# A decoder trunk's gate projections by seven products: first product seeded into the accumulating banks, Silu in one activation, two quarters by products in the last z pair

## Chip, cores and metric

The kernel runs on one core of a Trainium2 chip. The metric is the device time of one execution in microseconds (us), the median over several runs. The engines in the texts are TensorE (PE in the profile; its weight loads are PEld), VectorE (DVE), ScalarE (ACT), GpSimd (POOL, here above all the issuer of one DMA queue) and SyncE (SP, which issues the weight loads).

## What is computed

Two layers over 256 tokens of width 2048. The first mixes by a gated linear recurrence (HGRN2) and an RG-LRU, the second by an mLSTM. The change lies in the second layer: `og` and `z` are two 2048 x 2048 projections of the normalised input, which gate the mLSTM's output before its output projection.

```python
hn = rmsnorm(h, o_norm[j])
u = hn @ o_w_in[j]                     # q,k | v | og | z | ig | fg
...
yc = mlstm(q, k, v.reshape(bsz, s, C_HEADS, C_DV), li, lf)
yc = (head_rmsnorm(yc, c_norm[j]) * jax.nn.sigmoid(og.astype(jnp.float32))
      * jax.nn.silu(z.astype(jnp.float32)))
mix = yc.astype(h.dtype) @ o_w_out[j]
h = h + mix
pl = rmsnorm(p[i].astype(h.dtype) @ ple_w[i], ple_norm[i])
h = h + jax.nn.sigmoid(h @ ple_gate_w[i]) * pl
```

All of it is float32. A product of two float32 matrices is made of three passes: each operand is split into a high part and the rest (`hi`, `lo`), and hi x hi, hi x lo and lo x hi are added up in one PSUM bank.

## The kernel before

**Products.** A projection takes its output in blocks: 512 output columns (index `j`) by 128 tokens (index `hf`, two halves) fill one PSUM bank. The contraction over 2048 inputs is cut into four quarters (`kq`), each with a 128 x 2048 weight block that comes as two 512 KB pieces. A piece is loaded by an SP transfer into a `raw` buffer (five of them), cast to its high part `whi` on ScalarE (line 135, or 206 for pieces loaded elsewhere) and subtracted to its low part `wlo` on VectorE (line 136 or 207); there are four `whi` and four `wlo` buffers. A quarter for both token halves is 24 matmuls of 128 x 128 by 512 columns (`plain`, line 223).

**Seven products.** `seven` (line 262) makes two output blocks `j`, `j + 1` at once. For the quarters in `kqs` it treats the two token halves, the two input halves (`side`) and the two output blocks as a 2 x 2 by 2 x 2 matrix product and forms it with seven products in place of eight (Strassen's scheme in Winograd's form). The combinations of activations (`qs`, by `combos`) are made once beforehand; the combinations of weights are made in the call, in the buffers X, Y, Z (and W). With two quarters, X and Y are pairs of tiles from `chain2` (tag `qk`, four buffers), and the sums with a block still in DRAM are made by transfers on the POOL queue that add to the tile (`add_loaded`, line 288). With one quarter they are single tiles from `chain` (tag `ch`, two buffers) and the sums are VectorE additions (`add`). The quarters in `rest` go by `plain`. A product on one quarter has 6 matmuls, on two 12.

**Banks.** A call uses four PSUM banks: A, E and B from the pool `pm` (tag `mm`, three banks) and F from `px` (tag `mx`, three banks). The first product, A11 times B11, is part of all four outputs: A goes on accumulating into output (0, 0), and a copy of the product, `p1`, is kept in SBUF and added to or subtracted from what B, F and E hold later on, by `soon` on VectorE (line 292). `p15` and `g` are the other two SBUF halves that collect partial sums. The four results leave the generator one after another: (0, 0) from A, (0, 1) from `p15`, (1, 0) from `g`, (1, 1) from `p1`.

**Callers.** `pair` (line 1338) starts a call; its last argument says whether two quarters go by products. There are four calls in a row: og for blocks 0 and 1 (one quarter), og for blocks 2 and 3 (two), z for 0 and 1 (two), z for 2 and 3 (one). Each og result passes a Tanh on ScalarE (line 1349), which later multiplies the mLSTM's numerator (`mixed_gates`). Each z result passes a Tanh (line 1363) and a VectorE product (line 1364): (tanh(z/2) + 1) z is twice silu(z), and the factor 1/4 in `fac` (line 1298), with the norm's scale, makes up for both gates. Line 1368 multiplies with the mLSTM's result. When both halves of a block are there, `feature_major` (started as lane `fm0` to `fm3`) turns it: VectorE transposes (line 648), a transfer to DRAM and four back on the POOL queue (lines 635 and 638), then scaling and splitting. After the fourth call come the per-layer embedding (`embed`, matmuls of line 472) and the output projection, which reads what the lanes made.

**Order.** The program is written in one order and a planner orders each engine's instructions by priority and by when it expects their inputs. `high_priority(offset=n)` puts instructions as if written n places earlier: 400 for the weight splits and `add`, 450 for `soon` and the copy of A, 100 for the z gates. `pump` advances each lane by one step; it stands within `plain`, between the token halves, and at some places in `seven`. An instruction that waits holds up those behind it on its engine or queue.

Of the kernel before, what the change touches and what calls it, by code (L numbers as in the profile page):

```python
# [11 lines left out]
F32 = mybir.dt.float32  # L12
# [3 lines left out]
AF = mybir.ActivationFunctionType  # L16
ALU = mybir.AluOpType
PSUM = bass.MemoryType.PSUM

P = 128  # L20
# [23 lines left out]
def trunk(ctx: ExitStack, tc: tile.TileContext, a, out):  # L44
    nc = tc.nc
    v, s, gp, te, sy = nc.vector, nc.scalar, nc.gpsimd, nc.tensor, nc.sync
# [176 lines left out]
    def plain(w, j, kq, act, ps, first=(False, False), end=False):  # L223

        parts = load_weights(w[4 * j + kq])
        for hf in range(2):
            product(ps[hf], stationary(act, (2 * kq, 2 * kq + 1), hf), parts, first[hf], end)
            if hf == 0:
                pump()
# [32 lines left out]
    def seven(w, j, act, qs, kqs, room, part):  # L262

        def src(b, side, kq):
            return block(w[4 * (j + b) + kq], side * 1024, 1024)

        def load(tile_of, b, side):
            tiles = []
            for kq in kqs:
                t = tile_of()  # L270
                sy.dma_start(out=t, in_=src(b, side, kq))
                tiles.append(t)
            return tiles

        def ring():
            return wp.tile([P, 1024], F32, name="raw", tag="raw", bufs=5)

        def split(tiles):
            return [split_weights(t) for t in tiles]

        def add(x, y):
            with tc.high_priority(offset=400):
                for xi, yi in zip(x, y):
                    v.tensor_tensor(out=xi, in0=xi, in1=yi, op=ALU.add)

        def add_loaded(x):
            for xi, kq in zip(x, kqs):
                gp.dma_start(out=xi, in_=src(1, 0, kq), accum_op=ALU.add)

        def soon(out, in0, in1, op):  # L290
            with tc.high_priority(offset=450):
                v.tensor_tensor(out=out, in0=in0, in1=in1, op=op)

        def quadrant(side, hf):
            return stationary(act, [2 * kq + side for kq in kqs], hf)

        def combo(n):
            return [[t for kq in kqs for t in qs[n, kq][x]] for x in range(2)]

        two = len(kqs) == 2  # L300
        rest = [kq for kq in range(4) if kq not in kqs]
        A, E, B = (pm.tile([P, 512], F32, name="mm", tag="mm") for _ in range(3))
        F = px.tile([P, 512], F32, name="mx", tag="mx")
        p1, p15, g = part(), part(), part()
        X = load(room, 0, 0)
        product(A, quadrant(0, 0), split(X), True)
        if two:
            add_loaded(X)
        with tc.high_priority(offset=450):
            s.copy(p1, A)  # L310
        Y = load(room, 1, 1)
        product(E, combo(4), split(Y), True)
        if not two:
            W = load(ring, 1, 0)
            add(Y, W)
            add(W, X)
        plain(w, j, rest[0], act, (A, F), first=(False, True))
        product(B, combo(1), split(X if two else W), True)
        add(X, Y)
        if two:  # L320
            add_loaded(Y)
        soon(p15, B, p1, ALU.add)
        if not two:
            plain(w, j, rest[1], act, (A, F))
            product(B, combo(2), split(X))
            soon(g, B, p1, ALU.subtract)
        pump()
        Z = load(ring, 0, 1)
        product(A, quadrant(1, 0), split(Z))
        if not two:  # L330
            add(X, Z)
        plain(w, j, rest[-1], act, (A, F))
        yield 0, 0, A
        if two:
            product(B, combo(2), split(X))
            add(X, Z)
            soon(g, B, p1, ALU.subtract)
            product(F, quadrant(1, 1), split(X), end=True)
            pump()
        product(B, combo(3), split(Y))  # L340
        soon(p15, B, p15, ALU.subtract)
        if not two:
            product(F, quadrant(1, 1), split(X), end=True)
        soon(p15, F, p15, ALU.subtract)
        pump()
        yield 0, 1, p15
        for kq in rest:
            plain(w, j + 1, kq, act, (E, B), end=(kq == 3))
        soon(g, E, g, ALU.add)
        yield 1, 0, g  # L350
        soon(p1, B, p1, ALU.subtract)
        yield 1, 1, p1

    def newton(y, t, r, yh):
        v.tensor_scalar(t.bitcast(I32), y.bitcast(I32), 1, None, op0=ALU.logical_shift_right)
# [265 lines left out]
    norm = {}  # L621
# [506 lines left out]
    with tc.tile_pool(name="m1", bufs=2) as m1:  # L1128
# [156 lines left out]
        def mix_norm():  # L1285


            t, r, yh = (m1.tile([P, 16], F32, name=n, bufs=1) for n in ("nwt", "nwr", "nwy"))
            s.activation(den, den, AF.Abs)
            v.tensor_tensor(out=den.rearrange("p (h n) -> p h n", h=2), in0=den.rearrange("p (h n) -> p h n", h=2),  # L1290
                            in1=aT[:, 1, :, 0:8], op=ALU.max)
            v.tensor_scalar(den, den, 1e21, EPS ** 0.5, op0=ALU.min, op1=ALU.mult)
            v.tensor_tensor(out=den, in0=den, in1=den, op=ALU.mult)
            v.scalar_tensor_tensor(den, ss, 1.0 / 256, den, op0=ALU.mult, op1=ALU.add)
            newton(den, t, r, yh)
            for hf in range(2):
                c = slice(hf * 8, hf * 8 + 8)
                v.tensor_scalar(fac[:, c], r[:, c], norm["rt"][:, hf:hf + 1], 0.25, op0=ALU.mult, op1=ALU.mult)
            yield

        qs = {}
# [25 lines left out]
        def part():  # L1327
            n = len(turn) % 4
            turn.append(n)
            return store_of[n // 2][:, n % 2 * 512:(n % 2 + 1) * 512]  # L1330
# [7 lines left out]
        def pair(w, jj, two):  # L1338
            return seven(w, jj, acth, qs, (0, 1) if two else (0,), chain2 if two else chain, part)
# [17 lines left out]
        pact = load_p()  # L1357
        for jj in (0, 2):
            us = [m1.tile([P, 2, 512], F32, name="u", tag="vt", bufs=6) for _ in range(2)]
            for b, hf, src in pair(a["oz"], jj, not jj):  # L1360
                j, u = jj + b, us[b]
                with tc.high_priority(offset=100):
                    s.activation(u[:, hf], src, AF.Tanh, scale=norm["rth"][:, hf:hf + 1])
                    v.scalar_tensor_tensor(u[:, hf], u[:, hf], 1.0, src, op0=ALU.add, op1=ALU.mult)
                for i in range(2):
                    c = hf * 8 + 2 * j + i
                    e = slice(i * 256, (i + 1) * 256)
                    v.scalar_tensor_tensor(u[:, hf, e], u[:, hf, e], fac[:, c:c + 1], nums[j][:, hf, e],
                                           op0=ALU.mult, op1=ALU.mult)
                if hf:  # L1370
                    start(f"fm{j}", feature_major(u, "cn", 4 * j, y, 5))
# [114 lines left out]
        rest = last_chunk()  # L1486
# [153 lines left out]
```

## Time and profile before

| | us |
|---|---|
| median of 3 runs (1028.17 to 1028.58) | 1028.18 |
| profiled execution, whole time | 1028.08 |
| its span, first to last instruction | 1026.3 |
| TensorE busy | 1016.2 (99%) |
| VectorE busy | 794.4 (77%) |
| ScalarE busy | 623.1 (61%) |
| mean DMA rate over the span | 235 GB/s |
| mean granted TensorE clock | 0.997 |

The page's chain of work that ended last is 97% TensorE. Matmuls overlap: a row's duration (0.39 us) is longer than the distance between two starts, and a busy TensorE means that matmuls followed one another without a gap, not how fast they ran. Times in rows of a timeline are counted from the span's start. In brackets at a row's end stands how long the engine had been idle before it and which instruction ended that.

### The profile page before, as it was taken

Reading aid. Unit: us, or ns where it says so; the run is one execution under the profiler, and the core shown is the slowest. Engines: PE = TensorE matmul, PEld = TensorE weight load, DVE = VectorE, ACT = ScalarE, POOL = GpSimd, SP = SyncE. Lnnn points to the kernel's source line nnn. Section 1 sums busy time; section 2 is a strip of 40 time slices with the busy share of each in tenths; the row PEclk is TensorE's granted clock in tenths of the full one; section 3 lists DMA queues with packets and bytes.
Section 4 is the critical chain, followed back from the end, with each engine's and each line's share of the span. In section 5 each row is a group of like instructions: output and inputs, shape, how many; then the busy total and the mean of one; then the engine's idle time right before and its main releaser. Section 6 shows DMA issues by size and latency. Waiting matters only on the chain.

```text
span 1026.3 us, 14463 instructions
## 1 busy us (share of the span) xinstructions
PE 1016.2 (99%) x5194; PEld 843.8 (82%) x5194; DVE 794.4 (77%) x1180; ACT 623.1 (61%) x893; POOL 101.7 (10%) x186
## 2 busy tenths in 40 slices
PE   9999999999999999999999999999999999999996
PEld 7888888888888888888888888888888888888886
DVE  7858968969685775767559997888999986766684
ACT  7675554686974344565457876665666667344562
POOL 0111101011112121021021100000011112111000
PEclk9999999999999999999999999999999999999998
DMA  9887757567688897697798755376875789887652
GB/s 361 331 240 237 221 175 203 169 200 231 228 264 276 290 292 234 225 308 259 221 288 255 228 184 189 124 245 194 278 173 170 234 275 329 250 275 258 219 185 82
DMA packets 69384, 241.09 MB, mean 235 GB/s; under 512 B 8992, under 2 KB 10400, under 8 KB 69312
## 3 DMA queue, kind: packets, MB, share of 16 engines
q1 hardware_dynamic: 55008, 194.41, 58.0%
q0 software_dynamic: 13872, 45.23, 15.7%
q8 instruction: 40, 0.66, 0.3%
q10 hardware_dynamic: 432, 0.52, 0.1%
q14 instruction: 32, 0.26, 0.1%
HBM read 220.21 MB, written 19.92 MB: 234 GB/s over the span
## 4 chain that ended last, share of the span: by engine, by line
PE 97%; ACT 1%; DMA 1%; DVE 1%; issue 0%; ACTq 0%; DVEq 0%
PE mm L196 21%; PE mm L197 21%; PE mm L198 21%; PE mm L217 12%; PE mx L198 4%; PE mx L196 4%; PE mx L197 4%; PE mx L217 3%; PE nu L1276 1%; PE mm L472 1%; DMA raw<-in_pw_dram 1%; PE mm L1466 1%; PE mm L1464 1%; PE mm L1465 1%; PE mx L785 0%; DVE wlo L136 0%
## 5 line engine op out<-in xcount | busy, mean ns | idle before, releaser
L136 DVE TENSOR_TENSOR wlo<-raw,whi 128x1024 fp32r<-128x1024 f32 (+1 forms) x333 | 401.6, 1214 | 156.6 <-ACT whi L135 147.7
L135 ACT CAST whi<-raw 128x1024 fp32r<-128x1024 f32 (+1 forms) x333 | 348.1, 1048 | 268.0 <-PE mm L198 183.5
L196 PE MATMUL mm<-whi,ahl 128*128 128x512 f32 x960 | 375.1, 391 | 0.0
L197 PE MATMUL mm<-wlo,ahl 128*128 128x512 f32 x960 | 374.0, 390 | 0.2 <-DVE wlo L136 0.2
L198 PE MATMUL mm<-whi,ahl 128*128 128x512 f32 x960 | 373.6, 389 | 0.0
L196 PEld LDWEIGHTS mm<-whi,ahl 128*128 128x128 f32 x960 | 180.2, 188 | 38.1 <-issue 0.8
L197 PEld LDWEIGHTS mm<-wlo,ahl 128*128 128x128 f32 x960 | 180.2, 188 | 37.6 <-DVE wlo L136 0.9
L198 PEld LDWEIGHTS mm<-whi,ahl 128*128 128x128 f32 x960 | 180.3, 188 | 37.6
L217 PE MATMUL mm<-whi,ahl 128*128 128x512 f32 x288 | 91.1, 389 | 0.0
L217 PEld LDWEIGHTS mm<-whi,ahl 128*128 128x128 f32 x288 | 54.1, 188 | 11.2
L196 PE MATMUL mx<-whi,ahl 128*128 128x512 f32 x160 | 62.2, 389 | 0.0
L197 PE MATMUL mx<-wlo,ahl 128*128 128x512 f32 x160 | 62.2, 389 | 0.0
L198 PE MATMUL mx<-whi,ahl 128*128 128x512 f32 x160 | 62.2, 389 | 0.0
L217 PE MATMUL mm<-wlo,ahl 128*128 128x512 f32 x144 | 56.3, 391 | 0.3 <-DVE wlo L136 0.3
L207 DVE TENSOR_TENSOR wlo<-ch,whi 128x1024 fp32r<-128x1024 f32 x34 | 41.0, 1220 | 6.0 <-ACT whi L206 5.4
L206 ACT CAST whi<-ch 128x1024 fp32r<-128x1024 f32 x34 | 35.6, 1052 | 6.4 <-PE mm L217 3.4
L197 PEld LDWEIGHTS mx<-wlo,ahl 128*128 128x128 f32 x160 | 30.1, 188 | 6.3
L196 PEld LDWEIGHTS mx<-whi,ahl 128*128 128x128 f32 x160 | 30.1, 188 | 6.2
L198 PEld LDWEIGHTS mx<-whi,ahl 128*128 128x128 f32 x160 | 30.0, 188 | 6.2
L217 PE MATMUL mx<-whi,ahl 128*128 128x512 f32 x104 | 34.4, 390 | 0.0
L217 PEld LDWEIGHTS mm<-wlo,ahl 128*128 128x128 f32 x144 | 27.0, 188 | 6.5 <-DVE wlo L136 1.0
L217 PE MATMUL mm<-whi,q 128*128 128x512 f32 x96 | 32.1, 389 | 0.0
(370 smaller groups left out, 1110.7 us busy)
## 6 DMA issues: line engine op xcount, KB each, us to landing
raw<-in_ew_dram SPq DMA_DIRECT2D x64, 512.0 KB, 5.1
raw<-in_g_dram SPq DMA_DIRECT2D x64, 512.0 KB, 4.9
raw<-in_eo_dram SPq DMA_DIRECT2D x32, 512.0 KB, 5.5
raw<-in_oqk_dram SPq DMA_DIRECT2D x32, 512.0 KB, 4.8
raw<-in_ov_dram SPq DMA_DIRECT2D x32, 512.0 KB, 4.4
raw<-in_oo_dram SPq DMA_DIRECT2D x32, 512.0 KB, 4.9
raw<-in_oog_dram SPq DMA_DIRECT2D x24, 512.0 KB, 4.5
raw<-in_oz_dram SPq DMA_DIRECT2D x24, 512.0 KB, 4.7
```

The source lines that it names most:

```text
L135: last["act"] = s.copy(h, r).ins
L136: last["dve"] = v.tensor_tensor(out=l, in0=r, in1=h.bitcast(F32), op=ALU.subtract).ins
L196: te.matmul(ps[hf], xh, wh, start=(k == 0), stop=False)
L197: te.matmul(ps[hf], xh, wl, start=False, stop=False)
L198: last["pe"] = te.matmul(ps[hf], xl, wh, start=False, stop=(k == KT - 1)).ins
L206: last["act"] = s.copy(hi, r).ins
L207: last["dve"] = v.tensor_tensor(out=lo, in0=r, in1=hi.bitcast(F32), op=ALU.subtract).ins
L217: last["pe"] = te.matmul(o, x, y, start=(first and k + i == 0), stop=(end and k == n - 1 and i == 2), skip_group_check=True).ins
L472: last["pe"] = te.matmul(ps[hf][:, o:o + w_], tokens(pact[x], k, hf), (hi, lo)[y][:, k * 512 + o:k * 512 + o + w_], start=(n == mine[0]), ...
L1276: te.matmul(ps[:, 0:n], x[:, i, o:o + P], y[:, b, i], start=(b == 0 and x is sh and y is vh), stop=(b == hf and y is vl))
L1464: te.matmul(o, xh, wh, start=(k == 0), stop=False)
L1465: te.matmul(o, xh, wl, start=False, stop=False)
```

## The change

It has three parts.

- In `seven`, A moves to the pool `px`, and F, E and B take the three banks of `pm`. After the first product ScalarE copies A into F and its negative into B, and no later product starts those banks anew, so both go on accumulating on top. With that, `p1` is gone; `b5` (for `p15`) and `g` take plain copies of B on ScalarE (`keep`), two VectorE steps stay for `b5` and one for `g`, and result (1, 1) is read from B itself. This holds for all four calls.
- The z gates pass one Silu on ScalarE with the norm's scale in place of Tanh and the VectorE product; `fac` is set to half of `r`.
- The last call, z for blocks 2 and 3, puts two quarters through products in place of one.

```diff
@@ -291,6 +291,10 @@
+        def keep(out, bank):
+            with tc.high_priority(offset=450):
+                s.copy(out, bank)
@@ -299,31 +303,32 @@
-        A, E, B = (pm.tile([P, 512], F32, name="mm", tag="mm") for _ in range(3))
-        F = px.tile([P, 512], F32, name="mx", tag="mx")
-        p1, p15, g = part(), part(), part()
+        A = px.tile([P, 512], F32, name="mx", tag="mx")
+        F, E, B = (pm.tile([P, 512], F32, name="mm", tag="mm") for _ in range(3))
+        b5, g = part(), part()
...
         with tc.high_priority(offset=450):
-            s.copy(p1, A)
+            s.copy(F, A)
+            s.activation(B, A, AF.Copy, scale=-1.0)
...
-        plain(w, j, rest[0], act, (A, F), first=(False, True))
-        product(B, combo(1), split(X if two else W), True)
+        plain(w, j, rest[0], act, (A, F))
+        product(B, combo(1), split(X if two else W))
...
-        soon(p15, B, p1, ALU.add)
+        keep(b5, B)
...
-            soon(g, B, p1, ALU.subtract)
+            keep(g, B)
...
-        soon(p15, B, p15, ALU.subtract)
+        soon(b5, B, b5, ALU.subtract)
...
-        soon(p15, F, p15, ALU.subtract)
+        soon(b5, F, b5, ALU.subtract)
         pump()
-        yield 0, 1, p15
+        yield 0, 1, b5
...
-        soon(p1, B, p1, ALU.subtract)
-        yield 1, 1, p1
+        yield 1, 1, B
@@ -1295,7 +1299,7 @@
-                v.tensor_scalar(fac[:, c], r[:, c], norm["rt"][:, hf:hf + 1], 0.25, op0=ALU.mult, op1=ALU.mult)
+                v.tensor_scalar(fac[:, c], r[:, c], 0.5, None, op0=ALU.mult)
@@ -1357,11 +1361,10 @@
-            for b, hf, src in pair(a["oz"], jj, not jj):
+            for b, hf, src in pair(a["oz"], jj, True):
                 j, u = jj + b, us[b]
                 with tc.high_priority(offset=100):
-                    s.activation(u[:, hf], src, AF.Tanh, scale=norm["rth"][:, hf:hf + 1])
-                    v.scalar_tensor_tensor(u[:, hf], u[:, hf], 1.0, src, op0=ALU.add, op1=ALU.mult)
+                    s.activation(u[:, hf], src, AF.Silu, scale=norm["rt"][:, hf:hf + 1])
```

More of the change, by code (lines that the diff above doesn't have):

```diff
@@ L336, in seven @@
             add(X, Z)
-            soon(g, B, p1, ALU.subtract)
+            keep(g, B)
             product(F, quadrant(1, 1), split(X), end=True)
```

## The prediction

> **What bounds the kernel now.** I read the page's busy shares first, then the table of engines by stretch over the four `seven` calls and the embedding that follows them, then TensorE's timeline at the joints.
>
> ```profile
> PE 1016.2 (99%) x5194; PEld 843.8 (82%) x5194; DVE 794.4 (77%) x1180; ACT 623.1 (61%) x893; POOL 101.7 (10%) x186
> ```
>
> ```profile
> core 0: us, PE busy (x) PEld busy (x) DVE busy (x) ACT busy (x) POOL busy (x), PEclk, DMA share, GB/s
> 661.96:707.47 45.51, 45.51 (x216) 38.22 (x214) 39.83 (x67) 27.53 (x43) 1.77 (x2) 1.00 0.69 221
> 707.47:748.85 41.38, 41.09 (x181) 33.72 (x180) 36.22 (x35) 27.00 (x29) 3.37 (x4) 1.00 0.79 230
> 748.85:789.65 40.80, 40.80 (x181) 33.80 (x180) 40.30 (x43) 25.85 (x27) 2.25 (x3) 1.00 0.63 177
> 789.65:832.00 42.35, 42.35 (x187) 34.84 (x186) 39.14 (x49) 27.31 (x37) 5.55 (x10) 1.00 0.75 244
> 832.00:842.88 10.88, 10.88 (x49) 9.01 (x48) 10.85 (x16) 7.71 (x10) 2.18 (x4) 1.00 0.85 251
> ```
>
> The columns are length, then busy time with instruction count for each engine. The first four stretches are the calls in order: oog pair 0 (one quarter by products), oog pair 2 (two quarters), oz pair 0 (two), oz pair 2 (one). TensorE is busy throughout at a granted clock of 1.00, so the kernel's time is its count of matmuls times their pitch, plus the few places where it waits. VectorE is nearly as full (40.30 of 40.80 us in call 3); ScalarE is two thirds full. I found the joints in the timeline:
>
> ```profile
> 663.32 0.39 PE L217 MATMUL mm<-whi,q 128*128 128x512 f32 x1
> ...
> 664.68 0.39 PE L217 MATMUL mm<-whi,ahl 128*128 128x512 f32 x1
> ...
> 710.19 0.39 PE L217 MATMUL mm<-whi,q 128*128 128x512 f32 x1
> ...
> 751.57 0.39 PE L217 MATMUL mm<-whi,q 128*128 128x512 f32 x1
> ...
> 759.73 0.39 PE L217 MATMUL mm<-whi,q 128*128 128x512 f32 x1
> ...
> 791.01 0.39 PE L217 MATMUL mm<-whi,q 128*128 128x512 f32 x1
> ...
> 832.00 0.39 PE L472 MATMUL mx<-whi,ahl 128*128 128x512 f32 x1
> ```
>
> Each call's first `whi,q` row is the start of product E; product A stands before it with 6 matmuls (one quarter) or 12 (two). Call 3 holds 180 matmuls from 748.85 to 789.65: 40.80 / 180 = 0.2267 us each. That is the pitch; the 0.39 of a row is the pipelined length.
>
> **What each call loses now.** Call 4 has 186 matmuls, 42.16 us at that pitch, and takes 42.35: 0.19 lost. Call 2 has 180 and takes 41.38: 0.58 lost. Call 1 has 186 and the last `mix` products besides, so its loss can't be read off. Call 3 loses nothing. Call 2's loss has a row:
>
> ```profile
> 714.94 0.50 PE L217 MATMUL mm<-wlo,ahl 128*128 128x512 f32 x1 [0.29 <-DVE wlo L136]
> ```
>
> The late `wlo` was VectorE's last in an unbroken row of work:
>
> ```profile
> 708.52 1.23 DVE L207 TENSOR_TENSOR wlo<-ch,whi 128x1024 fp32r<-128x1024 f32 x1 [1.79 <-ACT whi L206]
> 709.66 0.68 DVE L292 TENSOR_TENSOR pr<-mm,pr 128x512 f32<-128x512 f32 x1
> 710.27 1.22 DVE L207 TENSOR_TENSOR wlo<-ch,whi 128x1024 fp32r<-128x1024 f32 x1
> 711.40 1.22 DVE L136 TENSOR_TENSOR wlo<-raw,whi 128x1024 fp32r<-128x1024 f32 x1
> 712.53 1.22 DVE L1343 SCALAR_TENSOR_TENSOR num<-tho,num 128x1024 f32<-128x1024 f32 x1
> 713.67 1.22 DVE L136 TENSOR_TENSOR wlo<-raw,whi 128x1024 fp32r<-128x1024 f32 x1
> ```
>
> **The change part by part.** *Seven products on two quarters in call 4.* One quarter: 7 products of 6 and 6 `plain` quarters of 24, 186. Two: 7 of 12 and 4 of 24, 180. Six matmuls go: 6 x 0.2267 = **1.36 us**, on TensorE, so on the path. Call 4 then has the form of call 3, whose loss is nil, so I also count its 0.19 as gone (bounds 0 and 0.19). It adds three weight splits (22 for 19), each one cast on ScalarE and one subtraction on VectorE, the costliest rows of the page:
>
> ```profile
> L136 DVE TENSOR_TENSOR wlo<-raw,whi 128x1024 fp32r<-128x1024 f32 (+1 forms) x333 | 401.6, 1214 | 156.6 <-ACT whi L135 147.7
> L135 ACT CAST whi<-raw 128x1024 fp32r<-128x1024 f32 (+1 forms) x333 | 348.1, 1048 | 268.0 <-PE mm L198 183.5
> ```
>
> So 3 x 1.05 = 3.1 us on ScalarE and 3 x 1.21 = 3.6 us on VectorE; the VectorE additions of weight tiles stay at four. It also reads two more 512 KB blocks (18 for 16), 1 MB in 41 us on top of 244 GB/s, about 270: the DMA share goes from 0.75 to some 0.83, and the stretch after it runs at 0.85 with TensorE full. Four of its transfers become accumulating ones on the POOL queue (the second rival). Its X and Y tiles now come from the ring of four that call 3 uses, and must wait for call 3's last splits; calls 2 and 3 share that ring in the same way today and the start of call 3 loses nothing.
>
> *First product into the banks.* Per call one ScalarE copy of A (L310) becomes two, and two of the six VectorE evictions (L292, `b5` and `g` by `keep`) become ScalarE copies; the last one, `p1 = B - p1`, goes altogether. VectorE loses 3 x 0.68 = 2.1 us per call, ScalarE gains 3 x 0.57 = 1.7 us, by these rows:
>
> ```profile
> L310 ACT COPY pr<-mm x4: 559/568/587, 663.7 to 791.5; 128x512 f32<-128x512 f32 x4
> L292 DVE TENSOR_TENSOR pr<-mm,pr x20: 650/684/692, 673.9 to 834.2; 128x512 f32<-128x512 f32 x20
> L1364 DVE SCALAR_TENSOR_TENSOR u<-u,pr x6: 681/687/694, 783.1 to 836.5; 128x512 f32<-128x512 f32 x6
> L1363 ACT ACTIVATE u<-pr,rth x6: 718/724/725, 782.4 to 834.9; 128x512 f32<-128x512 f32 x6
> ```
>
> No row has a copy from bank to bank; I take 0.57 (from bank to SBUF), between 0.47 (the spacing of two ScalarE starts below) and 0.72 (L1363, which reads SBUF and a scale). The Trainium skill, "ScalarE: Activation LUTs", under "Step-by-step: what each stage is for", says that ScalarE reaches PSUM with less latency than SBUF; by it each copy costs at most 0.57, and no run here shows it yet.
>
> In call 2 the eviction at 709.66 is the one that goes. Every later VectorE start moves up by its 0.61 us (709.66 to 710.27). The late `wlo` was due at 714.50, seven matmuls after 710.19 + 12 x 0.2267 = 712.91, and came 0.44 later; it is then in time. The 0.29 goes; the rest of the 0.58 is a slow restart behind it, so the gain is 0.3 to 0.58 and I take 0.3, the recorded idle time.
>
> *The new wait.* Bank A can't be added to until both copies have read it; behind the waiting matmul stands all of TensorE. Call 1 is the tight one, because E there has only 6 matmuls:
>
> ```profile
> 663.69 0.59 ACT L310 COPY pr<-mm 128x512 f32<-128x512 f32 x1
> 664.16 1.07 ACT L206 CAST whi<-raw 128x1024 fp32r<-128x1024 f32 x1
> ...
> 711.01 0.57 ACT L310 COPY pr<-mm 128x512 f32<-128x512 f32 x1
> ...
> 752.04 0.56 ACT L310 COPY pr<-mm 128x512 f32<-128x512 f32 x1
> ```
>
> The copies follow at 0.47 us (663.69 to 664.16), so the second would end at 664.16 + 0.59 = 664.75, and A's next matmul is due at 664.68: with a semaphore about 0.2 us late. I take **+0.2**, between 0 (F's copy is the only one) and 1.0 (a cast comes between the two). In call 2 the second copy ends at 712.05 and A is due at 712.91; in call 3 at 753.1 against 754.29. These wait for nothing.
>
> *One Silu for Tanh and a VectorE product.* Eight L1364 go, 8 x 0.69 = 5.5 us of VectorE over calls 3 and 4; ScalarE's count stays. Call 3 then has 40.30 - 2.1 - 2.8 = 35.4 us on VectorE, call 4 39.14 + 3.6 - 2.1 - 2.8 = 37.8 of 40.8, and ScalarE 27.3 + 3.1 + 1.7 = 32.1 at most. No VectorE time is on the path but in call 2, so I count nothing. The function is new to the kernel, so a table load comes with it; the trace has this one:
>
> ```profile
> 1018.20 1.28 ACT L1434 ACT_TABLE_LOAD   x1
> 1019.50 0.20 ACT L1434 ACTIVATE warm<-th 128x1 f32<-128x1 f32 x1
> ...
> 768.09 0.69 ACT L1363 ACTIVATE u<-mm,rth 128x512 f32<-128x512 f32 x1 [1.67 <-PE mm L217]
> ```
>
> The first z activation at 768.09 stands behind 1.67 us of idle ScalarE, which holds 1.28 us; cost nothing, and at most 1.28 if the load is held with its activation. Whether a second load follows for the later Tanh no row tells; I count it as covered too. The Trainium skill, "ScalarE: Activation LUTs", under "What ACT_TABLE_LOAD costs", speaks against this part: 1283 ns for the load, which the row confirms, and about 1380 ns of drain, which no row here shows (the next activation starts 1.30 us after the load did). By it a switch is 2.66 us, 1.0 us more than the idle time, and the sum would be 1.0 us higher if nothing else hid it.
>
> **Sum.** The profiled execution took 1028.08 us, 1026.3 of it the span; the three runs' median is 1028.18, so the two agree within 0.1. 1028.08 - 1.36 - 0.19 - 0.3 + 0.2 = **1026.4 us**. Past the calls TensorE's order is the same and the tail after its last matmul is untouched, so all of it arrives at the end.
>
> **The rivals.** *ScalarE hands it back.* If the planner puts a weight cast between the two copies of A, call 1 waits 1.0 and call 2 about 0.2 (711.01 + 0.47 + 0.95 + 0.57 = 713.0 against 712.91, and the semaphore). Against the forecast's +0.2 that is 1.0 more: **1027.4**, and up to 1028.2 with an exposed table load. For it: ScalarE runs back to back at 711 (the Tanh before the copy). Against: the copies have the higher priority.
>
> *The accumulation stuck on POOL (slower).* Call 4's X tiles are now added to by POOL transfers, and POOL's queue at that time also carries the first z pair's way through DRAM:
>
> ```profile
> 744.91 0.85 POOL L288 DMA_DIRECT2D ch<-in_oz_dram  x1 [24.11 <-DVE wlo L207]
> 746.26 0.84 POOL L288 DMA_DIRECT2D ch<-in_oz_dram  x1 [0.50 <-DVE wlo L207]
> ...
> 787.95 0.56 POOL L635 DMA_DIRECT2D ducn<-w  x1 [26.84 <-DVE w L648]
> 791.14 2.24 POOL L638 DMA_DIRECT2D r<-ducn  x4 [2.64 <-DMA ducn<-w]
> ```
>
> ```profile
> ch<-in_oz_dram POOLq DMA_DIRECT2D x4, 512.0 KB, 6.1
> hq<-dh POOLq DMA_DIRECT2D x4, 512.0 KB, 13.8
> ```
>
> Moved on by call 3's 40.8, the two accumulations are due at 785.7 and 787.1, a hair before L635. If the planner puts L635 and the four L638 ahead of them, they leave at 793.4 and land 6.1 us later, 799.5; cast 1.05 and subtraction 1.21 make 801.8. TensorE wants that tile at 759.73 + 40.8 = 800.5, so it waits 1.3, and 2.4 with the second tile, which lands 1.1 later: **1028.8**, slower than before. It is slower by more than 0.2% from landings of about 7.5 us on; at 13.8, which the queue's other row shows, it would be 1036. Against it: due times that let both accumulations go first.
>
> *More relief.* If both losses go whole (0.58 + 0.19) and call 1 doesn't wait, 1028.08 - 1.36 - 0.77 = **1025.95**, less what call 1 loses now.
>
> **How the numbers follow.** A measurement of this kernel can tell about 0.2%, 2.06 us, from no change: faster is below 1026.1, slower above 1030.2. The forecast has 0.56 with its own range 1025.9 to 1026.9, of which 0.24 lie below 1026.1 and 0.32 within. ScalarE's return has 0.18 (within), POOL's queue 0.15 (0.10 slower, 0.05 within), more relief 0.11 (faster). That makes faster 0.35, within 0.55, slower 0.10. The range 1025.6 to 1029.0 takes in all of these and the POOL case at its usual landing, with 0.35 under the case of more relief for call 1; about 0.15 stays outside.
>
> **What would show it.** Right: 5188 matmuls for 5194, calls 2 to 4 of 40.8 us, no wait at call 2's first `plain`, one more table load, no L1364 group, at most 0.3 us of wait on the ScalarE copy of A in call 1. Wrong: TensorE idle behind a `wlo` or a POOL transfer at call 4's B product; a call longer than its count times 0.2267; L638 ahead of L288 on POOL; or a length change outside 662 to 832.

## The result and the profile after

The changed kernel takes **1026.91 us** (median of 22 runs, 1026.11 to 1027.66) and the kernel before, run beside it, 1028.57 us (22 runs). The ratio is 0.9982, with a 95% interval of 0.9976 to 0.9989: a gain of 0.18%, which is within the 0.2% that counts as no change here, at the side of faster. The forecast was 1026.4.

The profiled execution of the changed kernel took 1026.88 us with a span of 1025.1 and a mean granted clock of 0.998. Its page has the busy shares:

```profile
PE 1015.3 (99%) x5188; PEld 843.8 (82%) x5188; DVE 787.6 (77%) x1163; ACT 632.2 (62%) x909; POOL 105.2 (10%) x190
```

There are 5188 matmuls, six fewer than before, as foreseen. The table of engines by stretch, over the same four calls and the embedding behind them:

```profile
core 0: us, PE busy (x) PEld busy (x) DVE busy (x) ACT busy (x) POOL busy (x), PEclk, DMA share, GB/s
661.90:708.54 46.64, 45.80 (x215) 38.14 (x214) 38.86 (x65) 28.94 (x46) 1.79 (x2) 1.00 0.63 194
708.54:749.58 41.04, 41.04 (x182) 33.67 (x180) 34.62 (x32) 28.09 (x32) 3.37 (x4) 1.00 0.80 231
749.58:790.38 40.80, 40.80 (x182) 33.80 (x180) 37.38 (x39) 28.55 (x31) 4.81 (x7) 1.00 0.84 243
790.38:831.18 40.80, 40.80 (x182) 33.80 (x180) 39.49 (x45) 31.62 (x42) 5.99 (x11) 1.00 0.83 229
831.18:842.06 10.88, 10.88 (x50) 9.01 (x48) 10.11 (x14) 7.17 (x10) 3.24 (x6) 1.00 0.94 271
```

The first number after the colon is the length. Set it against before: call 1 went from 45.51 to 46.64 (**+1.13**), call 2 from 41.38 to 41.04 (−0.34), call 3 stays at 40.80, call 4 went from 42.35 to 40.80 (**−1.55**). So calls 2 and 4 gained 1.9 us and call 1 gave 1.1 us back. The four calls together went from 170.04 to 169.28 us (661.90 to 831.18).

What TensorE waits for stands in the table of waits of this execution, and the joint itself in TensorE's timeline:

```profile
engine line waited for: us in total, times, longest us
PE mm L217 <- ACT mm L314: 0.8, 1, 0.8
```

```profile
663.04 0.39 PE L217 MATMUL mx<-whi,ahl 128*128 128x512 f32 x1
664.27 0.50 PE L217 MATMUL mm<-whi,ahl 128*128 128x512 f32 x1 [0.84 <-ACT mm L314]
664.61 0.40 PE L217 MATMUL mm<-whi,q 128*128 128x512 f32 x1
```

The first row is A's last matmul. The second is no part of E: it is the first matmul of `plain` into F, which the planner put ahead of product E (its first row, by the operand `q`, is the third). It adds to F and so waits for the copy of A into F (line 314), and E stands behind it. Note what a wait of "0.84" costs: the matmuls start 1.23 us apart instead of 0.23, because the row before still counts as busy after the next could have started, and 0.34 more pass until the third. Together 1.57 for two steps of 0.2267, so 1.12 us is lost, which is the whole growth of call 1.

The ScalarE copies and the last VectorE step of the projection before them:

```profile
663.63 0.59 ACT L314 COPY mm<-mx 128x512 f32<-128x512 f32 x1
664.14 0.57 ACT L315 ACTIVATE mm<-mx 128x512 f32<-128x512 f32 x1
```

```profile
663.50 0.74 DVE L1315 SCALAR_TENSOR_TENSOR vl<-mm,rcr,vt 128x512 fp32r<-128x512 f32 x1
```

The copies follow each other at 0.51 us and no cast comes between them. VectorE's `vl` reads the second half of the `ov` projection out of an `mm` bank until 663.50 + 0.74 = 664.24; this row matters in the experiments.

The other steps, in the timelines of ScalarE and of POOL:

```profile
767.17 1.28 ACT L1367 ACT_TABLE_LOAD   x1
768.82 0.69 ACT L1367 ACTIVATE u<-mx,rcr 128x512 f32<-128x512 f32 x1 [0.37 <-PE mx L217]
```

```profile
785.22 0.56 POOL L639 DMA_DIRECT2D ducn<-w  x1 [23.53 <-DVE w L652]
786.43 0.85 POOL L288 DMA_DIRECT2D ch<-in_oz_dram  x1 [0.65 <-DVE wlo L207]
787.79 0.84 POOL L288 DMA_DIRECT2D ch<-in_oz_dram  x1 [0.51 <-DVE wlo L207]
789.51 2.26 POOL L642 DMA_DIRECT2D r<-ducn  x4 [0.88 <-DMA ducn<-w]
```

The one new table load ends at 768.45, and then its activation still waits 0.37 for TensorE: it ran ahead of that wait, in idle time. (L639 and L642 are the lines 635 and 638 of before.) The accumulating transfers of call 4 leave between the transfer to DRAM and the four back.

Behind the calls, 0.4 us more was won than the calls explain: the last Tanh on ScalarE moved by 0.82, the end of the span by 1.2.

```profile
1017.80 0.38 ACT L1425 ACTIVATE th<-mm 128x256 f32<-128x256 f32 x1 [2.13 <-PE mm L1466]
```

```profile
1016.98 0.38 ACT L1428 ACTIVATE th<-mm 128x256 f32<-128x256 f32 x1 [2.13 <-PE mm L1469]
```

Before (first row) 8.5 us lie between that row and the end of the span, after (second row) 8.1. In all twelve experiments it is 8.1 where call 4 has two quarters by products and 8.5 where it has one. Only scaling and the output transfers lie there. Why the one should shorten the other no row tells; it stays open.

### The profile page after: what moved, and what is told of

Read it like the earlier page. It is cut to its first block, busy times and chain, and to the rows that moved or that the text cites. A ratio compares the mean times of both kernels' runs of the same rounds, so it can differ in the third digit from the quotient of the medians.

```text
span 1025.1 us, 14447 instructions
## 1 busy us (share of the span) xinstructions
PE 1015.3 (99%) x5188; PEld 843.8 (82%) x5188; DVE 787.6 (77%) x1163; ACT 632.2 (62%) x909; POOL 105.2 (10%) x190
## 5 line engine op out<-in xcount | busy, mean ns | idle before, releaser
L136 DVE TENSOR_TENSOR wlo<-raw,whi 128x1024 fp32r<-128x1024 f32 (+1 forms) x329 | 396.8, 1215 | 164.7 <-ACT whi L135 155.4
L196 PE MATMUL mm<-whi,ahl 128*128 128x512 f32 x960 | 375.1, 391 | 0.0
L197 PE MATMUL mm<-wlo,ahl 128*128 128x512 f32 x960 | 373.7, 389 | 0.0
L198 PE MATMUL mm<-whi,ahl 128*128 128x512 f32 x960 | 373.6, 389 | 0.0
L196 PEld LDWEIGHTS mm<-whi,ahl 128*128 128x128 f32 x960 | 180.2, 188 | 38.0 <-issue 0.8
L198 PEld LDWEIGHTS mm<-whi,ahl 128*128 128x128 f32 x960 | 180.2, 188 | 37.5
L197 PEld LDWEIGHTS mm<-wlo,ahl 128*128 128x128 f32 x960 | 180.3, 188 | 37.0
L217 PE MATMUL mm<-whi,ahl 128*128 128x512 f32 x244 | 77.9, 390 | 0.8 <-ACT mm L314 0.8
L196 PE MATMUL mx<-whi,ahl 128*128 128x512 f32 x160 | 62.2, 389 | 0.0
L198 PE MATMUL mx<-whi,ahl 128*128 128x512 f32 x160 | 62.2, 389 | 0.0
L207 DVE TENSOR_TENSOR wlo<-ch,whi 128x1024 fp32r<-128x1024 f32 x41 | 49.5, 1222 | 8.2 <-ACT whi L206 6.9
L217 PEld LDWEIGHTS mm<-whi,ahl 128*128 128x128 f32 x244 | 45.8, 188 | 10.6 <-ACT mm L314 1.3
L217 PE MATMUL mm<-wlo,ahl 128*128 128x512 f32 x122 | 47.5, 390 | 0.0
L206 ACT CAST whi<-ch 128x1024 fp32r<-128x1024 f32 x41 | 42.8, 1053 | 7.6 <-PE mm L217 5.4
L217 PE MATMUL mx<-whi,ahl 128*128 128x512 f32 x128 | 41.6, 389 | 0.0
L217 PE MATMUL mm<-whi,q 128*128 128x512 f32 x112 | 37.1, 389 | 0.0
L196 PEld LDWEIGHTS mx<-whi,ahl 128*128 128x128 f32 x160 | 30.0, 188 | 6.2
L198 PEld LDWEIGHTS mx<-whi,ahl 128*128 128x128 f32 x160 | 30.0, 188 | 6.2
L217 PEld LDWEIGHTS mx<-whi,ahl 128*128 128x128 f32 x128 | 24.0, 188 | 5.0
```

Source lines behind the costliest of these rows:

```text
L136: last["dve"] = v.tensor_tensor(out=l, in0=r, in1=h.bitcast(F32), op=ALU.subtract).ins
L196: te.matmul(ps[hf], xh, wh, start=(k == 0), stop=False)
L197: te.matmul(ps[hf], xh, wl, start=False, stop=False)
L198: last["pe"] = te.matmul(ps[hf], xl, wh, start=False, stop=(k == KT - 1)).ins
L206: last["act"] = s.copy(hi, r).ins
L207: last["dve"] = v.tensor_tensor(out=lo, in0=r, in1=hi.bitcast(F32), op=ALU.subtract).ins
```

## The experiments

The theory: call 4's six matmuls fewer and call 2's late `wlo` are the gain, and seeding F and B from ScalarE is what costs in call 1. The rivals: the gain is VectorE's relief, or the order in call 1 is to blame and not the seeding. Call lengths are read as above, from the start of A to the start of the next call's A.

### One part of the change at a time

`two_only` is the kernel before with this line alone:

```diff
-            for b, hf, src in pair(a["oz"], jj, not jj):
+            for b, hf, src in pair(a["oz"], jj, True):
```

> The kernel before with the last z pair on two quarters and nothing else. Theory (count and waits: the time is the matmuls times 0.2267 us plus TensorE's few waits): six matmuls fewer, 1.36 us, and call 4 without its 0.19 us of loss, so 1.4 to 1.6 us faster than before, ratio 0.9985, and call 4 takes 40.8 us. Rival (the parts lean on each other): without the VectorE work that the other two parts remove, call 4 needs 39.14 + 3.6 = 42.8 us of VectorE in 40.8 us, weight splits come late, TensorE waits 1 to 2 us in call 4 or in the embedding, and the time is that of before within 0.5 us.

Measured: 1026.68 us, ratio 0.9985 (0.9976 to 0.9994). Calls 3 and 4, by stretch:

```profile
748.87:789.67 40.80, 40.80 (x182) 33.78 (x180) 39.42 (x42) 25.86 (x27) 3.95 (x5) 1.00 0.79 232
789.67:830.47 40.80, 40.80 (x182) 33.78 (x180) 40.73 (x48) 28.56 (x34) 4.57 (x7) 1.00 0.80 228
```

Call 4 takes 40.80 with VectorE busy 40.73 of it: the gain of 1.55 needs none of the VectorE relief. The wait at call 2's `wlo` (0.29) is still there. The rival, a VectorE too full without the other two parts, falls.

`silu_only` is the kernel before with the Silu part alone (and `fac` to match):

```diff
-                    s.activation(u[:, hf], src, AF.Tanh, scale=norm["rth"][:, hf:hf + 1])
-                    v.scalar_tensor_tensor(u[:, hf], u[:, hf], 1.0, src, op0=ALU.add, op1=ALU.mult)
+                    s.activation(u[:, hf], src, AF.Silu, scale=norm["rt"][:, hf:hf + 1])
```

> The kernel before with Silu in the z gates and nothing else. Theory: the eight VectorE products were beside the path and the table load stands in ScalarE's idle time, so the time stays within 0.3 us of before (ratio 0.9997 to 1.0003). Rival 1 (relief of VectorE is worth something): 0.5 us or more faster. Rival 2 (the table load is on the path): 1 to 1.3 us slower.

Measured: 1027.95 us, ratio 0.9997 (0.9989 to 1.0006); the calls 169.97, 0.07 less. Eight VectorE products fewer are worth nothing that the medians can show. Inside the calls there is a little: call 4 takes 42.16 for 42.35, which is its 186 matmuls at the pitch, while call 2 takes 41.51 for 41.38.

`seed_only` is the changed kernel with those two parts taken back (and `fac` with them):

```diff
-            for b, hf, src in pair(a["oz"], jj, True):
+            for b, hf, src in pair(a["oz"], jj, not jj):
...
-                    s.activation(u[:, hf], src, AF.Silu, scale=norm["rt"][:, hf:hf + 1])
+                    s.activation(u[:, hf], src, AF.Tanh, scale=norm["rth"][:, hf:hf + 1])
+                    v.scalar_tensor_tensor(u[:, hf], u[:, hf], 1.0, src, op0=ALU.add, op1=ALU.mult)
```

> The kernel before with the first product seeded into F and B in all four calls and nothing else. Theory: call 1 pays about 1.1 us for the matmul of F that stands ahead of product E and waits for the ScalarE copy of A; call 2 gets back 0.3 us; the rest is unchanged: 0.6 to 0.8 us slower than before (ratio 1.0007). Rival (the seeding pays by the VectorE evictions that it removes): 0.3 us or more faster than before.

Measured: 1029.83 us, ratio **1.0015** (1.0006 to 1.0024). It is slower than the kernel before by 1.2 us, where 0.6 to 0.8 was expected. Call 1 takes 46.65 and call 2 41.02, as in the changed kernel, and call 4, which again has one quarter, 43.55 for 42.35:

```profile
791.17 0.39 PE L217 MATMUL mx<-whi,ahl 128*128 128x512 f32 x1
792.65 0.50 PE L217 MATMUL mm<-whi,ahl 128*128 128x512 f32 x1 [1.09 <-ACT mm L314]
...
796.63 0.39 PE L217 MATMUL mm<-whi,q 128*128 128x512 f32 x1
```

The same wait in the other one-quarter call, here with E far behind. So seeding costs 1.1 to 1.2 us in each one-quarter call and gives 0.36 in call 2. In the changed kernel call 4, which has two quarters and the Silu, is spared; no run separates these two, but calls 2 and 3 of `seed_only` have two quarters without the Silu and show no such wait.

### Is it the order in call 1?

`order` holds F's `plain` back until E's matmuls are issued, and changes nothing else:

```diff
-        plain(w, j, rest[0], act, (A, F))
+        with tc.issue_after(last["pe"]):
+            plain(w, j, rest[0], act, (A, F))
```

> The changed kernel with the matmuls of the first plain quarter held behind product E on TensorE; only one matmul of call 1 changes its place. Theory: the 1.0 us wait of call 1 goes and at most 0.2 us comes back as A's first matmul waits for the second copy; call 1 takes 45.5 to 45.8 us for 46.6, and the kernel is 0.8 to 1.0 us faster than the changed one, 2.4 to 2.8 us faster than before (ratio 0.9975). Rival (whatever order, bank A is read by ScalarE twice before it can go on): A's first matmul waits as long as F's did, and the time is that of the changed kernel within 0.3 us.

Measured: 1026.92 us, ratio 0.9985 (0.9977 to 0.9994). The expectation failed: E is first now, and waits as long, for something else.

```profile
662.85 0.39 PE L217 MATMUL mx<-whi,ahl 128*128 128x512 f32 x1
664.10 0.50 PE L217 MATMUL mm<-whi,q 128*128 128x512 f32 x1 [0.86 <-DVE vl L1316]
```

```profile
663.30 0.75 DVE L1316 SCALAR_TENSOR_TENSOR vl<-mm,rcr,vt 128x512 fp32r<-128x512 f32 x1
```

E starts when `vl` has read its bank (663.30 + 0.75 = 664.05). The pool `mm` has three banks, and the projection that ends at call 1's start still holds one of them until then. So the planner's order isn't the cause: without it the same time is lost. In the changed kernel two waits end together there, F's for the copy (663.63 + 0.59 = 664.22) and E's for `vl` (664.24), and putting off the one leaves the other. The time is the one that the rival expected, but its wait didn't come: A's next matmul follows E without a gap.

### Is it the bank of A and F?

`banks` gives call 1 its former banks, A in `mm` and F in `mx`, still seeded by ScalarE; `banks_order` adds the hold of `order`. In both, a part of the first product is missing from the results, by all appearance in F, the one seeded tile whose bank differs from the changed kernel's; why, no run here tests. Every matmul and copy is still there.

```diff
-        A = px.tile([P, 512], F32, name="mx", tag="mx")
-        F, E, B = (pm.tile([P, 512], F32, name="mm", tag="mm") for _ in range(3))
+        one, three = (px, pm) if two else (pm, px)
+        A = one.tile([P, 512], F32, name="mx" if two else "mm", tag="mx" if two else "mm")
+        F = three.tile([P, 512], F32, name="mm" if two else "mx", tag="mm" if two else "mx")
+        E, B = (pm.tile([P, 512], F32, name="mm", tag="mm") for _ in range(2))
```

> The changed kernel with call 1's banks as before, but the planner's order: one matmul of F still stands ahead of product E, and it needs ScalarE's copy of A. Theory: it waits for the copy's end as in the changed kernel, at about 664.2; call 1 takes 46.4 to 46.7 us. Rival (only the late bank counts): call 1 takes 45.5 to 45.8 us.

> The changed kernel with call 1 alone (one quarter) keeping the old banks, A in the pool mm and F in mx, and the first plain quarter held behind product E. Theory (call 1 waits for a bank: F, E and B all want one of three mm banks at once, and the third is the one that the last v projection still holds until VectorE's vl at 664.1): E gets the bank that has been free for 2 us, B alone takes the late one, no wait before E, and at most 0.2 us before A goes on. Call 1 takes 45.5 to 45.8 us for 46.6, the kernel is 0.9 to 1.1 us faster than the changed one. Rival (bank A read by ScalarE twice is the limit): the wait moves to A's next matmul, call 1 stays at 46.4 to 46.7.

Measured: `banks`, a single run, 1026.96 us, with the old wait of 0.84 for the copy into F at F's first matmul, and the calls 169.10. `banks_order` 1026.9 us, ratio 0.9984 (0.9975 to 0.9993), the calls 169.21. The expected gain of about a microsecond failed again:

```profile
663.44 0.39 PE L217 MATMUL mm<-whi,ahl 128*128 128x512 f32 x1
664.70 0.50 PE L217 MATMUL mm<-whi,q 128*128 128x512 f32 x1 [0.87 <-DVE vl L1318]
```

E waits for `vl` although F no longer asks for an `mm` bank. What is left of the seeding here is the copy into B, which stands ahead of E and so asks for a bank before E does. In the kernel before, B's bank is first asked for by B's own product, long after E. The read of the same half of `ov`, before (first row) and in `banks_order` (second row):

```profile
663.55 0.74 DVE L1311 SCALAR_TENSOR_TENSOR vl<-mm,rcr,vt 128x512 fp32r<-128x512 f32 x1
```

```profile
663.90 0.74 DVE L1318 SCALAR_TENSOR_TENSOR vl<-mm,rcr,vt 128x512 fp32r<-128x512 f32 x1
```

In the kernel before E starts at 663.32 (its row stands in the prediction), ahead of this read, so E's bank isn't the one that `vl` reads; nor is A's, which is being written since 661.96. Of the three banks `vl`'s was left for B. In `banks_order` A, E and B are again the three in `mm`, and E starts as `vl` ends (663.90 + 0.74 = 664.64). So E and B have changed banks: B has the one that was free, E the late one.

### Without seeding, and with it only where two quarters go by products

`no_seed` is the kernel before with the edits of `two_only` and `silu_only` together; `after_again` is the changed kernel, on the same chip.

> The kernel before with two quarters in the last z pair and Silu, without the seeding. Theory (the seeding costs call 1 1.13 us and brings call 2 0.34): calls 1 and 2 as before, calls 3 and 4 of 40.8 us; 1.5 us faster than before (ratio 0.9985) and 0.7 to 0.8 us faster than the changed kernel of the same chip. Rival (the seeding brings what the medians showed): slower than the changed kernel by 0.2 us or more.

> The changed kernel unaltered, on the chip of the next three. Theory (count and waits): its four calls are 0.8 us shorter than before (-1.36 and -0.19 in call 4, -0.34 in call 2, +1.13 in call 1), so ratio 0.9992. Rival (the medians of the first comparison, 1.7 us, are right and the calls' lengths don't tell the whole gain): ratio 0.9982 to 0.9985.

Measured: `no_seed` **1026.24** us, ratio 0.9977 (0.9967 to 0.9986); the changed kernel 1026.71, ratio 0.9983 (0.9974 to 0.9992). The changed kernel is 0.47 slower than itself without the seeding by the medians, whose intervals overlap, and 0.55 by the calls (169.15 us against 168.60). From 0.7 to 0.8 was expected; call 1 lost its 1.13 as before, but call 2's gain was larger in this pair (40.91 against 41.49). The expectation of `after_again` failed: the calls' lengths alone made the ratio 0.9992, and 0.9983 came, as its rival had it. The medians differ by 1.9 us on this chip too, more than the calls explain. Of call 2's wait `no_seed` shows the cause of before:

```profile
714.55 0.50 PE L217 MATMUL mm<-wlo,ahl 128*128 128x512 f32 x1 [0.37 <-DVE wlo L136]
```

`mixed` is the changed kernel with call 1 written as before: every seeded line stands under `if two`, the former one under `else`.

```diff
...
+            if two:
                 s.copy(F, A)
                 s.activation(B, A, AF.Copy, scale=-1.0)
+            else:
+                s.copy(p1, A)
...
```

> The changed kernel, with the first product written into F and B only in the calls that take two quarters by products (2, 3 and 4); the one-quarter call 1 is written as before. Theory (seeding costs only where E is short, and pays in call 2): call 1 goes back to 45.5 us with no wait on a ScalarE copy, call 2 keeps its 41.04 us without the 0.29 wait, calls 3 and 4 stay at 40.8, so the four calls take 168.2 us, 1.0 to 1.1 under the changed kernel's 169.3 and 0.3 to 0.4 under the 168.6 of the kernel without seeding; the time is then 1025.8 to 1026.2. Rival (the planner's order in call 2 rests on call 1's): call 1 or 2 takes up the difference again and the calls take 168.6 or more.

> The kernel without seeding once more, beside the mixed one: calls 168.6 us as before, time 1026.2 with a spread of 0.3. If the mixed kernel's theory holds, this one is 0.3 to 0.4 us slower than it.

Measured: 1026.33 us for `mixed` (ratio 0.9971, 0.996 to 0.9983) and 1026.31 for `no_seed` (0.9973, 0.9962 to 0.9984). The stretches of `mixed`, calls 1 and 2:

```profile
661.99:707.50 45.51, 45.51 (x215) 38.21 (x214) 39.73 (x67) 27.74 (x43) 1.79 (x2) 1.00 0.63 199
707.50:748.66 41.16, 41.16 (x181) 33.63 (x180) 35.12 (x33) 28.04 (x31) 3.36 (x4) 1.00 0.80 230
```

Call 1 is back at 45.51, so its loss was the seeding there and nothing else; call 2 keeps a part of its gain (41.16 for 41.35 in `no_seed` beside it). The calls take 168.27 us against 168.46, near the 168.2 that was expected. This 0.2 us is less than the medians can show, which are equal, and the time of 1025.8 to 1026.2 was just missed; both kernels are ahead of the two that were compared first.

### What the rival on POOL would have cost

`pool` is the changed kernel with the two accumulating transfers of call 4's X tiles held behind the four L642 transfers (L645 here):

```diff
             for xi, kq in zip(x, kqs):
-                gp.dma_start(out=xi, in_=src(1, 0, kq), accum_op=ALU.add)
+                with ExitStack() as behind:
+                    if w is a["oz"] and j == 2 and x is X:
+                        behind.enter_context(tc.issue_after(last["hop"]))
+                    gp.dma_start(out=xi, in_=src(1, 0, kq), accum_op=ALU.add)
```

> The changed kernel with the two accumulating transfers of call 4's X tiles put behind the four L642 transfers on the POOL queue, as the prediction's rival had it. They should leave at about 791.8 and 792.9 instead of 786.4 and 787.8. The B product of call 4 needs the first split tile at about 801.3. With landings of about 6 us the second split is ready at 801.4 and TensorE waits 0 to 0.3 us; with the 13.8 us of that queue's other row it waits 6 to 8 us. The rival was priced at 2.4.

```profile
789.45 2.24 POOL L645 DMA_DIRECT2D r<-ducn  x4 [3.54 <-DMA ducn<-w]
791.68 1.84 POOL L291 DMA_DIRECT2D ch<-in_oz_dram  x2
```

```profile
797.60 1.05 ACT L206 CAST whi<-ch 128x1024 fp32r<-128x1024 f32 x1 [2.15 <-DMA ch<-in_oz_dram]
802.09 1.05 ACT L206 CAST whi<-ch 128x1024 fp32r<-128x1024 f32 x1 [3.44 <-DMA ch<-in_oz_dram]
```

Call 4 takes 43.30 us for 40.80, **2.5** more (a single run, 1029.53 us in all). The first tile is cast 5.9 us after its transfer left, the second, whose transfer left 0.9 later, only at 802.09. The landing lay between the two that were expected. The rival of the prediction priced this at 2.4 and had the mechanism right; that the price fits is in part luck, since it had the second tile landing 1.1 after 799.5. It didn't come about in the changed kernel because the planner let both transfers go ahead of the four.

### How far ScalarE covers table loads

`tables` is the changed kernel with an Exp on one column ahead of each of the eight Silu rows, which changes the table each time:

```diff
+                    s.activation(m1.tile([P, 1], F32, name="swap", tag="swap", bufs=1), src[:, 0:1], AF.Exp, scale=0.0)
                     s.activation(u[:, hf], src, AF.Silu, scale=norm["rt"][:, hf:hf + 1])
```

> The changed kernel with a 128x1 Exp ahead of each of the eight Silu rows, which changes the table and back: some 16 more table loads of 1.28 us. Theory (ScalarE has room, a load there is covered): TensorE waits for none of the first pair's loads, and the span grows by less than 1 us, at the places where ScalarE runs back to back. Rival (a table change costs a drain besides, 2.7 us in all): the eight loads of each call take 21 us of ScalarE's 41, ScalarE falls behind and the span grows by 10 us or more.

It has fourteen table loads more. Of its fifteen, four lie in call 3, eight in call 4 and three behind it. The two calls by stretch:

```profile
749.87:790.67 40.80, 40.80 (x182) 33.78 (x180) 36.33 (x36) 30.58 (x34) 3.11 (x4) 1.00 0.79 230
790.67:835.79 45.12, 42.48 (x181) 33.46 (x180) 38.82 (x43) 40.73 (x52) 7.73 (x12) 1.00 0.76 218
```

Both expectations missed: the span grew by 5.3 us (a single run, 1032.21 us), 5.0 of it behind the start of call 4. Call 3 hides its four loads whole. Call 4 has 10.3 us of loads on a ScalarE that is already busy 31.6 of 40.8, and takes 4.3 more. No drain shows behind a load: in the rows below the Silu starts 1.29 us after its load did.

```profile
799.33 1.28 ACT L1368 ACT_TABLE_LOAD   x1
800.62 0.69 ACT L1368 ACTIVATE u<-mm,rcr 128x512 f32<-128x512 f32 x1
```

```profile
801.36 0.50 PE L217 MATMUL mm<-whi,q 128*128 128x512 f32 x1 [0.51 <-ACT u L1368]
```

The last row is E of call 4. It waits until that Silu has read result (1, 1) of call 3, which the change leaves in the bank B instead of in SBUF. It is the same shortage of `mm` banks as in call 1, from another holder.

## Why the prediction was nearly right

The kind of result was right, no change with a lean to faster, and the bound too: TensorE's count of matmuls times their pitch, plus its few waits. By their size three of the four terms held, one of them in part by luck, and one was much too small. Of the signs that it named for being wrong two came, calls 1 and 2 longer than their counts and a change behind 832 (0.4 at the end); of those for being right two failed, call 2 at 41.04 for 40.8 and a wait of 0.84 on the copy of A for at most 0.3.

- **Seven products on two quarters, −1.36 and call 4's loss, −0.19.** Right: 1.55 in the changed kernel and 1.55 in `two_only`. Call 4 is 180 matmuls at the pitch, nothing lost.
- **Call 2's late `wlo`, −0.3.** The number came, 0.34, but only half of the path. The wait is there in `two_only` and both runs of `no_seed`, and TensorE's tables of waits name none in call 2 of the seeded kernels. 0.24 of the call's 0.58 stays, and VectorE's, the weight loads' and TensorE's rows of the changed kernel show where:

```profile
711.86 1.22 DVE L1347 SCALAR_TENSOR_TENSOR num<-tho,num 128x1024 f32<-128x1024 f32 x1
713.00 2.36 DVE L136 TENSOR_TENSOR wlo<-raw,whi 128x1024 fp32r<-128x1024 f32 x2
```

```profile
714.27 0.19 PEld L217 LDWEIGHTS mx<-wlo,ahl 128*128 128x128 f32 x1 [0.30 <-DVE wlo L136]
```

```profile
714.00 0.39 PE L217 MATMUL mx<-whi,ahl 128*128 128x512 f32 x1
714.27 0.50 PE L217 MATMUL mx<-wlo,ahl 128*128 128x512 f32 x1
714.61 0.64 PE L217 MATMUL mx<-whi,ahl 128*128 128x512 f32 x2
```

The second piece's `wlo` is done 6.8 us into the call instead of 7.4, in time, as foreseen. But the planner now puts `num` ahead of both pieces, and the first piece's `wlo` (713.00 + 1.22 = 714.22) comes just as it is due. Its weight load waits 0.30, and the 12 matmuls of this token half take 2.94 us (714.00 to 716.94) for 2.72. So what stays isn't the old wait's slow restart but a new and smaller wait behind the same engine, and that the term came out at its lower bound is luck. It also changes from execution to execution: call 2 takes 40.82 to 41.08 in the eight traces that seed all calls and 41.35 to 41.51 in the five that seed none. `mixed`, at 41.16, still has the eviction on VectorE ahead of the late `wlo` (709.48), since that is call 1's last step; so how much of the gain is the eviction, no run separates.
- **The new wait in call 1, +0.2.** This is the step that failed: it measured **+1.13**, above the upper bound of 1.0. The step looked at "A's next matmul" behind two copies. A wasn't what was late. The copy into B, and the one into F, claim `mm` banks at the start of the call, when the projection before it still reads one of them; what then waits is E, or, with the planner's order, F's first matmul ahead of E. Shown are that the loss goes when call 1 isn't seeded (`mixed`), that holding the order only moves it (`order`), and that E then starts as `vl` lets go of a bank (`order`, `banks_order`). That B's claim came ahead of E's follows from the rows of `vl` and E in the kernel before and in `banks_order`, since there are only three banks. What a version that writes B only after E would gain isn't shown: none was run, and F's first matmul would still wait for the copy unless E stands ahead of it. The first part of the change listed F, E and B in one pool of three banks, and the prediction took over the bank plan without asking who held those banks at 663.
- **Silu, 0.** Right by `silu_only`. One load more, none back for the Tanh that follows, and it sat in the idle time. The Trainium skill's page "ScalarE: Activation LUTs", under "What ACT_TABLE_LOAD costs", gives 1283 ns for a load, which all rows here confirm, and about 1380 ns of drain, by which the sum would have been 1.0 us higher; no row shows the drain, neither here nor at the loads of `tables`. The cover that the prediction named is finite: eight loads in call 4 cost 4.3.
- **VectorE's relief, 0.** Right for the forecast, and at its sharpest in `two_only`, where VectorE is busy 40.73 of 40.80 us in call 4 and TensorE waits for nothing in it. But that no VectorE time was on the path outside call 2 is wrong: the 0.19 that call 4 lost before was a late `wlo` too, by this weight load of the kernel before, and in `silu_only` it is gone (42.16).

```profile
792.87 0.19 PEld L217 LDWEIGHTS mm<-wlo,ahl 128*128 128x128 f32 x1 [0.31 <-DVE wlo L136]
```

- **The copies' durations.** The prediction took 0.57 us for a copy from bank to bank; the groups of the changed kernel have 578 ns for both forms:

```profile
L314 ACT COPY mm<-mx x4: 570/578/589, 663.6 to 793.3; 128x512 f32<-128x512 f32 x4
L315 ACT ACTIVATE mm<-mx x4: 562/578/589, 664.1 to 793.8; 128x512 f32<-128x512 f32 x4
```

- The Trainium skill's page "ScalarE: Activation LUTs", under "Step-by-step: what each stage is for", has PSUM as the destination with less latency for ScalarE. The copies from a bank to SBUF had 568 ns in the kernel before (L310) and 590 in the changed one (L296), on either side of the 578, so these rows neither show it nor speak against it.
- **The rivals.** ScalarE put no cast between the copies (663.63 and 664.14), so that rival's mechanism fell, though its time, 1027.4, is as near to the result as the forecast's. POOL's didn't happen and was priced about right. More relief fell too: call 2 kept 0.24 of its loss and call 1 waited.
- **The sum.** Call by call the profiled executions differ by +1.13, −0.34, 0 and −1.55; A of call 1 starts 0.06 earlier, and about 0.4 comes from behind the last Tanh. That is 1.2 us, from 1028.08 to 1026.88, where the forecast had 1.65. The medians differ by 1.66, but only by chance is that the forecast's number: the kernel before had medians of 1028.57 to 1028.72 in the comparisons, 0.5 above the profiled execution that was the prediction's base. What makes up these 0.5 stays open, with one trace of that kernel; executions differ by as much ahead of the calls, where A of call 1 starts between 661.47 and 662.31 us in the fourteen traces. The call lengths show what the medians hide, 0.9 that was missed in call 1 and 0.4 at the end that wasn't foreseen.

## What to carry to other kernels

Writing a partial result into an accumulating bank in place of keeping it in SBUF moves the claim on that bank forward to the time of the copy. Before doing so, list for each bank of the pool who holds it at that moment and when its last reader ends; a vector engine's relief is worth nothing if a matmul engine that is 99% busy then waits for a bank. And when a wait has been ascribed to the order of two instructions, exchange them: if the loss stays, a second wait ends at the same time, and its holder has to be found.

## What the runs showed of the hardware that wasn't expected

- A recorded wait costs more on TensorE than its bracket says: 0.84 us of idle time meant 1.12 us lost, since starts are 0.2267 apart while a row lasts 0.39, and the step after a wait took 0.34.
- A late operand can cost TensorE time that its own table of waits doesn't list: where a weight load waited 0.30 us for `wlo` (714.27), 12 matmuls took 2.94 us for 2.72, and where one waited 0.31 (792.87 before), call 4 lost 0.19.
- A table load can run ahead of the wait of the activation that needs it: at 767.17 it started 1.65 us before that activation, which after the load still waited 0.37 us for TensorE.
- Two accumulating 512 KB transfers that left POOL's queue 0.9 us apart, behind four small ones, were used 4.5 us apart (797.60 and 802.09 in `pool`).
